# Three 256-column matmuls per step for the feature-major products, and gate products issued one column group early

## The chip, the cores and the metric

The kernel runs on one NeuronCore of a Trainium2 chip. The metric is the time of one execution on the device in microseconds (us); several executions give a median. Engines as the profile names them: PE is TensorE's matmul, PEld its weight load, DVE is VectorE, ACT is ScalarE, POOL is GpSimd, SP is SyncE (here it issues the DMAs of the weights). PSUM is the memory that matmuls write to, SBUF the one that all engines work in.

## The reference

One layer of a decoder trunk with four parallel branches, 256 positions (S), 2048 features (D), float32, and a final norm:

```python
h = rmsnorm(x, norm_g)
proj = jnp.einsum('bsd,df->bsf', h, w_in)            # 2048 x 18432
ya = stick_breaking_attention(a_q, a_k, a_v) * silu(a_g)
yb = conformer_conv(b_a, b_b, ...) * silu(b_g)
yc = spatial_gating(gelu(c_u), gelu(c_v), ...) * silu(c_g)
yd = dilated_mixture(d_q, d_k, d_v) * silu(d_g)
yproj = jnp.einsum('bsnc,ncd->bsnd', stack(ya, yb, yc, yd), w_branch)
gates = sigmoid(jnp.einsum('bsd,df->bsf', h, w_gate) + b_gate)
x = x + jnp.einsum('bsd,de->bse', sum(gates * yproj), w_out)
return rmsnorm(x, final_g)
```

The input projection has 14 column groups, named a_q, a_k and so on; each branch is 1024 wide. The gate has a 2048-column group for each branch.

## The kernel before

**Precision.** Large products run on numbers split in two: `hi` is the value rounded to the matmul's format (a ScalarE copy, L130), `lo` the rest (a VectorE subtraction, L131). A product is `hi*hi + lo*hi + hi*lo`, three terms added up in PSUM. Activations are split once (`xhl` holds h with its 256 hi columns beside its 256 lo columns; `y` likewise for a branch), weights as they arrive.

**Weights.** `weight_plan` lists 258 tiles of 128 x 2048 in the order of use. `next_weights` loads the next one (SP queue, three landing buffers) and splits it in two halves into five `hi` and five `lo` buffers, with a priority 300 instructions ahead of its place. A half is freed by the last matmul that reads it.

**Two kinds of product.** *Feature-major* (`unit_t`, `mm_t`): weights are the stationary operand, h the moving one, and the result has features on partitions. For each of 16 steps k, L245 multiplies the hi weights with all 512 columns of `xhl` (hi and lo of h), and L248 the lo weights with its 256 hi columns. A tile `ps` takes two such products in a 512-column half each; `evac` (L264) adds the two 256-column parts of each half, by a ScalarE copy (L266) and a VectorE addition (L267). 120 weight tiles go this way. *Token-major* (`mm_n`, L286 to L288): h or y is stationary, 512 weight columns move, and positions are on partitions. This is used for the value groups (`proj_n`), the gates (`psg`), the branch products (`psy`) and the output.

**Stages.** In order: d_v (`proj_v`, on x not yet normalized, with `make_h` producing h between its two column halves c=0 and c=1); b_a and b_b with the convolution, whose taps VectorE works off in the background; the dilated attention; then `gate_proj("d")`, b_g, `gate_proj("b")`, a_v and the stick-breaking attention, `gate_proj("a")`, c_v, c_u and c_g, `gate_proj("c")`, the output product and the final norm. `gate_proj` has four column groups c of 512; for each it makes the gate product (a bias matmul L369, then 96 matmuls), its sigmoid (L375), the branch product (48 matmuls), and multiplies and adds into `merged` (L382 to L385).

**Work put off.** `later(n, fn)` runs `fn` at the n-th next `tick()`; small steps of attention heads, and `sink` (transposes of a finished column group of `merged` into the operands `mh`, `ml` of the output product, L637), are emitted in the middle of later products in this way. `flush()` emits all that is pending at once.

**Order and buffers.** Python emits instructions in program order; a planner then orders each engine's instructions by priority and a simulated time, and gives tiles their buffers. A tile is freed when all that read or write it are done, and an engine takes its instructions in the planned order. PSUM has room for eight 512-column tiles: `ps_mm` two buffers of two (all large products), `ps_2` one buffer of two (`psy`, the norm's `pp`, attention's `po` and `cc`), `ps_s` two of one.

`make_h` (L213) uses `ps_2`: L225 and L226 sum the squares, L181 to L190 make `rstd`, sixteen L230 scale x, `split` makes `xhl`, L234 turns `rstd` into a column and L235 copies it out of `pp`.

Of the kernel before, what the change touches and what calls it, by code (L numbers as in the profile page):

```python
# [30 lines left out]
           c_u=7168, c_v=8192, c_g=9216, d_q=10240, d_k=13312, d_v=16384, d_g=17408)  # L31
BRANCH = dict(a=0, b=1, c=2, d=3)


def weight_plan():

    plan = []

    def t(name, i):
        plan.append(("in", OFF[name] // P + i))  # L40

    def n(name):
        for c in range(2):
            for q in range(4):
                plan.append(("inN", OFF[name] // 512 + c, q))

    def gate(b):
        for c in range(4):
            for q in range(4):
                plan.append(("gateN", BRANCH[b] * 4 + c, q))  # L50
            for q in range(2):
                plan.append(("brN", BRANCH[b], c, q))

    n("d_v")
    for i in range(8):
        t("b_a", i)
        t("b_b", i)
    for h in range(0, NH, 2):
        t("d_g", h)
        t("d_g", h + 1)  # L60
        for hh in (h, h + 1):
            for g in range(3):
                t("d_q", 8 * g + hh)
                t("d_k", 8 * g + hh)
    gate("d")
    for i in range(8):
        t("b_g", i)
    gate("b")
    n("a_v")
    for h in range(0, NH, 2):  # L70
        t("a_g", h)
        t("a_g", h + 1)
        for hh in (h, h + 1):
            t("a_q", hh)
            t("a_k", hh)
    gate("a")
    n("c_v")
    for i in range(8):
        t("c_u", i)
        t("c_g", i)  # L80
    gate("c")
    for c in range(4):
        for q in range(4):
            plan.append(("out", c, q))
    return plan
# [9 lines left out]
def hybrid_block(ctx: ExitStack, tc, w, x, xT, vec, bg, cst, dmask, sgu_wT, sgu_lg, sgu_lb, sgu_b, final_g, out):  # L95
# [11 lines left out]
    sc_p = ctx.enter_context(tc.tile_pool(name="sc", bufs=3))  # L107
    sm_p = ctx.enter_context(tc.tile_pool(name="sm", bufs=4))
    gt_p = ctx.enter_context(tc.tile_pool(name="gt", bufs=2))
    ps_mm = ctx.enter_context(tc.tile_pool(name="psm", bufs=2, space=bass.MemoryType.PSUM))  # L110
    ps_2 = ctx.enter_context(tc.tile_pool(name="ps2", bufs=1, space=bass.MemoryType.PSUM))
    ps_s = ctx.enter_context(tc.tile_pool(name="pss", bufs=2, space=bass.MemoryType.PSUM))

# [19 lines left out]
    def next_weights(expect, his=None, los=None):  # L133

        st = load_weights(expect)
        res = []
        for c in range(2):
            hi = his[c] if his else sp_p.tile([P, 1024], F32R, tag="hi", name="hi")[:]
            lo = los[c] if los else sp_p.tile([P, 1024], F32R, tag="lo", name="lo")[:]
            with tc.high_priority(SPLIT_AHEAD):  # L140
                split(hi, lo, st[:, c * 1024:(c + 1) * 1024])
            res.append((hi, lo))
        return res
# [3 lines left out]
    def later(n, fn):  # L147

        pending.append([n, fn])
# [11 lines left out]
    def flush():  # L161
        while pending:
            tick()
# [71 lines left out]
        V.tensor_copy(rstd_n[:], psn[:, 0:2])  # L235


    def mm_t(ps, j, weights, rhs, nk):

        for k in range(nk):  # L240
            hi, lo = weights[k // 8]
            o = (k % 8) * P

            def full(start, stop):
                T.matmul(ps[:, j, :], hi[:, o:o + P], rhs[:, k, :], start=start, stop=stop)  # L245

            def half():
                T.matmul(ps[:, j, 0:S], lo[:, o:o + P], rhs[:, k, 0:S], start=False, stop=False)  # L248

            if k < nk - 1:  # L250
                full(k == 0, False)
                half()
            else:
                half()
                full(False, True)

    def unit_t(e0, e1):
        ps = ps_mm.tile([P, 2, 512], F32, tag="mm", name="ps")
        mm_t(ps, 0, next_weights(e0), xhl, KD)
        mm_t(ps, 1, next_weights(e1), xhl, KD)  # L260
        tick()
        return ps

    def evac(ps, dst):  # L264
        bt = ev_p.tile([P, 2, S], F32, tag="bt", name="bt")
        A.activation(bt[:], ps[:, :, S:2 * S], AF.Copy)  # L266
        V.tensor_add(dst, ps[:, :, 0:S], bt[:])  # L267

    def ft(name, i):
        return ("in", OFF[name] // P + i)  # L270

    def proj_t(e0, e1):
        ps = unit_t(e0, e1)
        dst = qk_p.tile([P, 2, S], F32, tag="qk", name="dst")
        evac(ps, dst[:])
        return dst

    def mm_n(ps, weights, k0, lh, first, last, tbs=(0, 1)):
# [36 lines left out]
        return res  # L315

    def proj_n(name, c, step=None, first=False):
        ps = ps_mm.tile([P, 2, 512], F32, tag="mm", name="psn")
        for q in range(4):
            e = ("inN", OFF[name] // 512 + c, q)  # L320
            wts = first_weights(q, e) if first and c == 0 else next_weights(e)
            mm_n(ps, wts, 4 * q, xu_lh if first else x_lh, q == 0, q == 3)
            if q % 2:
                tick()
            if step is not None:
                step()
        if first and c == 0:
            make_h()
        return ps
# [25 lines left out]
        A.activation(bgr[:], b[:], AF.Copy)  # L355
        V.tensor_sub(bgr[32:64, :], b[32:64, :], bgr[32:64, :].bitcast(F32))

    def gate_proj(b, y, first=False, sink=None, step=None):

        bi = BRANCH[b]  # L360

        def y_lh(k, part, tb):
            return y[:, k, part * S + tb * P:part * S + (tb + 1) * P]

        for c in range(4):
            g = bi * 4 + c
            ps = ps_mm.tile([P, 2, 512], F32, tag="mm", name="psg")
            for tb in range(2):
                T.matmul(ps[:, tb, :], sel[:, g:g + 1].to_broadcast([P, P]), bgr[:], start=True, stop=False)  # L369
            for q in range(4):  # L370
                mm_n(ps, next_weights(("gateN", g, q)), 4 * q, x_lh, False, q == 3)
                if q % 2:
                    tick()
            gt = gt_p.tile([P, 2, 512], F32, tag="gt", name="gt")
            A.activation(gt[:], ps[:], AF.Sigmoid)  # L375
            psy = ps_2.tile([P, 2, 512], F32, tag="a2", name="psy")
            for q in range(2):
                mm_n(psy, next_weights(("brN", bi, c, q)), 4 * q, y_lh, q == 0, q == 1)
            tick()
            m = merged[:, :, c * 512:(c + 1) * 512]  # L380
            if first:
                V.tensor_mul(m, psy[:], gt[:])  # L382
            else:
                V.tensor_mul(gt[:], psy[:], gt[:])
                V.tensor_add(m, m, gt[:])  # L385
            if sink is not None:
                later(1, lambda c=c: sink(c))
            if step is not None:
                step()


    vd = proj_v("d_v", first=True)
# [80 lines left out]
            later(1, lambda g=g, qk=qk, qs=qs: scores(g, qk, qs))  # L473

    for h0 in range(0, NH, 2):
        sg = proj_t(ft("d_g", h0), ft("d_g", h0 + 1))
        A.activation(sg[:], sg[:], AF.Silu)
        conv(9)
        d_head(h0, sg)
        d_head(h0 + 1, sg)  # L480
# [24 lines left out]
                         scale=vec_sb[:, V_LG + i:V_LG + i + 1])  # L505

    conv_norm()
    flush()
    gate_bias()
    merged = big.tile([P, 2, D], F32, tag="m16", name="merged")  # L510
    gate_proj("d", yd, first=True)
# [2 lines left out]

    yb = new_y()
    for i in range(0, 8, 2):
        bg = proj_t(ft("b_g", i), ft("b_g", i + 1))
        A.activation(bg[:], bg[:], AF.Silu)
        V.tensor_mul(bg[:], bg[:], cv[:, i:i + 2, :])
        put_y(yb, i, 2, bg[:])  # L520

    flush()
    gate_proj("b", yb)


# [4 lines left out]
    ya = new_y()  # L530

    def a_pair(h0):
        sg = proj_t(ft("a_g", h0), ft("a_g", h0 + 1))
        A.activation(sg[:], sg[:], AF.Silu)
        zm = sc_p.tile([P, 2, 384], F32, tag="e1", bufs=1, name="zm")
        sph = sc_p.tile([P, 2, 384], F32R, tag="e3", bufs=1, name="sph")
        spl = sc_p.tile([P, 2, 384], F32R, tag="e4", bufs=1, name="spl")
# [41 lines left out]
    for h0 in range(0, NH, 2):  # L579
        a_pair(h0)  # L580

    flush()
    gate_proj("a", ya)


# [37 lines left out]
        put_y(yc, i, 1, ug[:, 0:1, :])  # L623

    for i in range(8):
        ug = proj_t(ft("c_u", i), ft("c_g", i))
        A.activation(ug[:, 0, :], ug[:, 0, :], AF.Gelu_apprx_tanh)
        A.activation(ug[:, 1, :], ug[:, 1, :], AF.Silu)
        later(2, lambda i=i, ug=ug: c_mix(i, ug))

    flush()


    mh = [t8_p.tile([P, KB, S], F32R, tag="t8", name=f"mh{i}") for i in range(2)]
    ml = [t8_p.tile([P, KB, S], F32R, tag="t8", name=f"ml{i}") for i in range(2)]

    def sink(c):  # L637
        pt = ps_mm.tile([P, 4, S], F32, tag="mm", name="pt")
        for f in range(4):
            for tb in range(2):  # L640
                o = c * 512 + f * P
                T.transpose(pt[:, f, tb * P:(tb + 1) * P], merged[:, tb, o:o + P], ident)
        ks = slice(4 * (c % 2), 4 * (c % 2) + 4)
        A.activation(mh[c // 2][:, ks, :], pt[:], AF.Copy)
        V.tensor_sub(ml[c // 2][:, ks, :], pt[:], mh[c // 2][:, ks, :].bitcast(F32))

    gate_proj("c", yc, sink=sink)
    flush()


    fg = y_p.tile([P, D], F32, tag="y", name="fg")
# [33 lines left out]
            (nc.scalar if c % 2 else nc.sync).dma_start(out[tb * P:(tb + 1) * P, cs], r[:, tb, cs])  # L685

    for c in range(3):
        ps = ps_mm.tile([P, 2, 512], F32, tag="mm", name="pso")
        for q in range(4):
            mm_n(ps, next_weights(("out", c, q)), 4 * q, m_lh, q == 0, q == 3)  # L690
        for tb in range(2):
            finish(c, ps, tb)
# [2 lines left out]
        wts.append(next_weights(("out", 3, q), his=[wh[:, q, 0, :], wh[:, q, 1, :]],  # L695
                                los=[sp_p.tile([P, 1024], F32R, tag="hi", name="wl")[:] for _ in range(2)] if q < 2 else None))
    for tb in range(2):
        ps = ps_mm.tile([P, 2, 512], F32, tag="mm", name="pso")
        for q in range(4):
            mm_n(ps, wts[q], 4 * q, m_lh, q == 0, q == 3, tbs=(tb,))  # L700
        finish(3, ps, tb)
        store(tb)
# [62 lines left out]
```

## Time and profile before

| | |
|---|---|
| median of 3 executions | 1505.41 us (1504.37 to 1506.78) |
| profiled execution | 1508.27 us, its span 1506.6 us |
| TensorE clock granted, mean | 0.994 |
| DMA | 280.47 MB, mean 186 GB/s |
| matmuls | 7484 |

The profile is of one execution and its times are in us from the start of the span. The first part gives each engine's busy time. "Idle before" is the time an engine stood still ahead of an instruction, with what ended it behind an arrow. Matmuls are pipelined: an entry's duration runs on while the next is already streaming, so the distance from start to start is what a matmul costs.

### The profile page before, as it was taken

The page shows a single profiled execution, that of the slowest core. Times are in us where ns is not written, and L with a number is a line of the kernel's source. Part 1 is how long each engine was busy: PE and PEld are TensorE (multiplying, and loading weights), DVE is VectorE, ACT ScalarE, POOL GpSimd, SP SyncE. Part 2 cuts the span into 40 slices and gives each one's busy share as a digit, 9 for nine tenths or more (in the row PEclk, how much of TensorE's full clock was granted, in tenths as well). Part 3 has the DMA queues.
Part 4 walks back from the last instruction along what each step waited for, and adds up shares of the span by engine and source line. Part 5 has one row for each costly group of instructions (what it writes and reads, how often), then busy time and mean ns, then how long its engine had stood idle before and what let it go on. Part 6 is the DMA issues. An engine that isn't in the chain of part 4 may idle for free.

```text
span 1506.6 us, 18648 instructions
## 1 busy us (share of the span) xinstructions
PE 1479.1 (98%) x7484; PEld 1255.4 (83%) x7484; DVE 944.4 (63%) x1249; ACT 760.2 (50%) x860; POOL 10.2 (1%) x22
## 2 busy tenths in 40 slices
PE   7999999999999999999999999999999999999997
PEld 5888888888888788888888888887888888888786
DVE  8899999866566754555545455554545666555454
ACT  7644445564454644454444466654444667444352
POOL 0000000000000000000000000000000000000000
PEclk9999999999999999999999999999999999999999
DMA  8555554445444555555555545444555555555562
GB/s 302 211 195 184 180 187 177 169 166 191 173 168 170 201 203 186 192 195 189 186 186 195 194 168 172 168 177 154 196 195 195 181 183 198 200 190 177 192 217 84
DMA packets 41318, 280.47 MB, mean 186 GB/s; under 512 B 4784, under 2 KB 4784, under 8 KB 8592
## 3 DMA queue, kind: packets, MB, share of 16 engines
q1 hardware_dynamic: 38880, 272.00, 50.5%
q0 software_dynamic: 1632, 6.24, 1.3%
q8 instruction: 58, 0.95, 0.3%
q10 hardware_dynamic: 720, 1.06, 0.2%
q14 instruction: 28, 0.23, 0.0%
HBM read 277.18 MB, written 2.10 MB: 185 GB/s over the span
## 4 chain that ended last, share of the span: by engine, by line
PE 97%; ACT 1%; DVE 1%; DMA 1%; issue 0%; DVEq 0%; ACTq 0%
PE ps L245 30%; PE ps L248 15%; PE psg L286 8%; PE psg L288 8%; PE psg L287 8%; PE psy L286 4%; PE psy L288 4%; PE psy L287 4%; PE psn L287 3%; PE psn L288 3%; PE psn L286 3%; PE pso L286 2%; PE pso L287 2%; PE pso L288 2%; DMA xt<-in_xT_dram 0%; PE psg L369 0%
## 5 line engine op out<-in xcount | busy, mean ns | idle before, releaser
L131 DVE TENSOR_TENSOR lo<-st,hi 128x1024 fp32r<-128x1024 f32 (+1 forms) x506 | 616.0, 1219 | 460.7 <-ACT hi L130 459.2
L130 ACT ACTIVATE hi<-st 128x1024 fp32r<-128x1024 f32 (+1 forms) x506 | 533.4, 1056 | 671.7 <-PE ps L245 262.3
L245 PE MATMUL ps<-xhl,hi 128*128 128x512 f32 x1920 | 675.5, 398 | 0.0
L248 PE MATMUL ps<-xhl,lo 128*128 128x256 f32 x1920 | 519.5, 281 | 0.0
L245 PEld LDWEIGHTS ps<-xhl,hi 128*128 128x128 f32 x1920 | 355.2, 188 | 74.6
L248 PEld LDWEIGHTS ps<-xhl,lo 128*128 128x128 f32 x1920 | 362.3, 189 | 9.6
L286 PE MATMUL psg<-hi,xhl 128*128 128x512 f32 x512 | 201.0, 393 | 1.1 <-ACT hi L130 1.1
L288 PE MATMUL psg<-hi,xhl 128*128 128x512 f32 x512 | 200.3, 391 | 0.0
L287 PE MATMUL psg<-lo,xhl 128*128 128x512 f32 x512 | 200.2, 391 | 0.0
L286 PEld LDWEIGHTS psg<-hi,xhl 128*128 128x128 f32 x512 | 96.4, 188 | 21.6 <-ACT hi L130 1.7
L288 PEld LDWEIGHTS psg<-hi,xhl 128*128 128x128 f32 x512 | 96.6, 189 | 20.2
L287 PEld LDWEIGHTS psg<-lo,xhl 128*128 128x128 f32 x512 | 96.6, 189 | 20.0
L412 DVE SCALAR_TENSOR_TENSOR cv<-glu,vec_sb,cv 128x255 f32<-128x255 f32 (+26 forms) x240 | 100.8, 463 | 0.2
L286 PE MATMUL psy<-hi,y 128*128 128x512 f32 x256 | 99.6, 389 | 0.0
L287 PE MATMUL psy<-lo,y 128*128 128x512 f32 x256 | 99.6, 389 | 0.0
L288 PE MATMUL psy<-hi,y 128*128 128x512 f32 x256 | 99.6, 389 | 0.0
L288 PEld LDWEIGHTS psy<-hi,y 128*128 128x128 f32 x256 | 48.1, 188 | 10.0
L287 PEld LDWEIGHTS psy<-lo,y 128*128 128x128 f32 x256 | 48.1, 188 | 10.0
L286 PEld LDWEIGHTS psy<-hi,y 128*128 128x128 f32 x256 | 48.1, 188 | 9.9
L286 PE MATMUL psn<-hi,xhl 128*128 128x512 f32 x128 | 49.8, 389 | 0.0
L287 PE MATMUL psn<-lo,xhl 128*128 128x512 f32 x128 | 49.8, 389 | 0.0
L288 PE MATMUL psn<-hi,xhl 128*128 128x512 f32 x128 | 49.8, 389 | 0.0
(207 smaller groups left out, 1105.2 us busy)
## 6 DMA issues: line engine op xcount, KB each, us to landing
st<-in_w_dram SPq DMA_DIRECT2D x254, 1024.0 KB, 4.8
xr<-in_x_dram POOLq DMA_DIRECT2D x8, 256.0 KB, 3.9
xt<-in_xT_dram SPq DMA_DIRECT2D x3, 512.0 KB, 8.7
st<-in_w_dram SPq DMA_DIRECT2D x4, 256.0 KB, 5.3
st<-in_w_dram SPq DMA_DIRECT2D x2, 512.0 KB, 7.4
fg<-in_final_g_dram POOLq DMA_DIRECT2D x1, 1024.0 KB, 6.8
out_dram<-r SPq DMA_DIRECT2D x4, 256.0 KB, 3.2
out_dram<-r ACTq DMA_DIRECT2D x4, 256.0 KB, 3.5
```

The lines of the kernel that those rows point to most:

```text
L130: A.activation(hi, src, AF.Copy)
L131: V.tensor_sub(lo, src, hi.bitcast(F32))
L245: T.matmul(ps[:, j, :], hi[:, o:o + P], rhs[:, k, :], start=start, stop=stop)
L248: T.matmul(ps[:, j, 0:S], lo[:, o:o + P], rhs[:, k, 0:S], start=False, stop=False)
L286: T.matmul(ps[:, tb, :], lh(k0 + kk, 0, tb), hi[:, o:o + 512], start=st, stop=False)
L287: T.matmul(ps[:, tb, :], lh(k0 + kk, 0, tb), lo[:, o:o + 512], start=False, stop=False)
L288: T.matmul(ps[:, tb, :], lh(k0 + kk, 1, tb), hi[:, o:o + 512], start=False, stop=sp)
L412: V.scalar_tensor_tensor(dst, src, wc, dst, op0=ALU.mult, op1=ALU.add)
```

## The change

- **Feature-major products.** Each step k is now three 256-column matmuls (hi weights with h's hi columns, hi weights with its lo columns, lo weights with its hi columns) that all add into the same 256 columns. Both products of a unit stand in one tile of 2 x 256 columns, from a new pool `ps_t` with two buffers. The sum is complete in PSUM, so one ScalarE pass evacuates it, with SiLU or GELU where one is wanted.
- **PSUM.** `ps_mm` goes from two buffers to one. Large token-major products alternate between `ps_mm` and `ps_2`: the second column half of `proj_n`, all `psy`, and every other output product take `ps_2`.
- **Gates.** `gate_proj` goes through `GATE_ORDER`: gate products g run one column group ahead of branch products y, and `sink` s stands at places of its own; the weight plan follows that order. The `flush()` calls around the gates are gone.
- **Transposes.** `sink` works in two parts of four transposes with tiles from `ps_t`; the one for the last column group is called in the first output product, ahead of its last quarter.

```diff
+GATE_ORDER = [(e[0], int(e[1])) for e in "g0 g1 y0 g2 s0 y1 g3 s1 y2 y3 s2".split()]
...
-    ps_mm = ctx.enter_context(tc.tile_pool(name="psm", bufs=2, space=bass.MemoryType.PSUM))
+    ps_t = ctx.enter_context(tc.tile_pool(name="pst", bufs=2, space=bass.MemoryType.PSUM))
+    ps_mm = ctx.enter_context(tc.tile_pool(name="psm", bufs=1, space=bass.MemoryType.PSUM))
...
+    def mm_t(ps, weights, rhs):
+
+        for k in range(KD):
             hi, lo = weights[k // 8]
             o = (k % 8) * P
...
+            T.matmul(ps, hi[:, o:o + P], rhs[:, k, 0:S], start=k == 0, stop=False)
+            T.matmul(ps, hi[:, o:o + P], rhs[:, k, S:2 * S], start=False, stop=False)
+            T.matmul(ps, lo[:, o:o + P], rhs[:, k, 0:S], start=False, stop=k == KD - 1)

     def unit_t(e0, e1):
-        ps = ps_mm.tile([P, 2, 512], F32, tag="mm", name="ps")
-        mm_t(ps, 0, next_weights(e0), xhl, KD)
-        mm_t(ps, 1, next_weights(e1), xhl, KD)
+        ps = ps_t.tile([P, 2, S], F32, tag="t", name="ps")
+        mm_t(ps[:, 0, :], next_weights(e0), xhl)
+        mm_t(ps[:, 1, :], next_weights(e1), xhl)
...
-    def proj_t(e0, e1):
+    def proj_t(e0, e1, funcs=(AF.Copy,)):
+
         ps = unit_t(e0, e1)
         dst = qk_p.tile([P, 2, S], F32, tag="qk", name="dst")
-        evac(ps, dst[:])
+        if len(funcs) == 1:
+            A.activation(dst[:], ps[:], funcs[0])
+        else:
+            for j in range(2):
+                A.activation(dst[:, j, :], ps[:, j, :], funcs[j])
...
     def proj_n(name, c, step=None, first=False):
-        ps = ps_mm.tile([P, 2, 512], F32, tag="mm", name="psn")
+        ps = (ps_2.tile([P, 2, 512], F32, tag="a2", name="psn") if c else
+              ps_mm.tile([P, 2, 512], F32, tag="mm", name="psn"))
...
+        def gate(c):
             g = bi * 4 + c
             ps = ps_mm.tile([P, 2, 512], F32, tag="mm", name="psg")
...
+            gts[c] = gt_p.tile([P, 2, 512], F32, tag="gt", name="gt")
+            A.activation(gts[c][:], ps[:], AF.Sigmoid)
+
+        def branch(c):
             psy = ps_2.tile([P, 2, 512], F32, tag="a2", name="psy")
...
+        for s, c in GATE_ORDER:
+            if s != "s":
+                (gate if s == "g" else branch)(c)
+            elif sink is not None:
+                sink(c)
...
     def sink(c):
-        pt = ps_mm.tile([P, 4, S], F32, tag="mm", name="pt")
...
+        for f0 in (0, 2):
+            pt = ps_t.tile([P, 2, S], F32, tag="t", name="pt")
...
     for c in range(3):
-        ps = ps_mm.tile([P, 2, 512], F32, tag="mm", name="pso")
+        ps = (ps_2 if c % 2 else ps_mm).tile([P, 2, 512], F32, tag="a2" if c % 2 else "mm", name="pso")
         for q in range(4):
+            if c == 0 and q == 3:
+                sink(3)
             mm_n(ps, next_weights(("out", c, q)), 4 * q, m_lh, q == 0, q == 3)
```

More of the change, by code (lines that the diff above doesn't have):

```diff
@@ L47, in gate @@
     def gate(b):
[L48 to L52, printed above, removed]
+        for s, c in GATE_ORDER:
+            if s == "g":
+                for q in range(4):
+                    plan.append(("gateN", BRANCH[b] * 4 + c, q))
+            elif s == "y":
+                for q in range(2):
+                    plan.append(("brN", BRANCH[b], c, q))
     n("d_v")
@@ L235, in make_h @@
         V.tensor_copy(rstd_n[:], psn[:, 0:2])
-    def mm_t(ps, j, weights, rhs, nk):
-        for k in range(nk):
+    def mm_t(ps, weights, rhs):
+        for k in range(KD):
             hi, lo = weights[k // 8]
             o = (k % 8) * P
[L244 to L255, printed above, removed]
+            T.matmul(ps, hi[:, o:o + P], rhs[:, k, 0:S], start=k == 0, stop=False)
+            T.matmul(ps, hi[:, o:o + P], rhs[:, k, S:2 * S], start=False, stop=False)
+            T.matmul(ps, lo[:, o:o + P], rhs[:, k, 0:S], start=False, stop=k == KD - 1)
     def unit_t(e0, e1):
-        ps = ps_mm.tile([P, 2, 512], F32, tag="mm", name="ps")
-        mm_t(ps, 0, next_weights(e0), xhl, KD)
-        mm_t(ps, 1, next_weights(e1), xhl, KD)
+        ps = ps_t.tile([P, 2, S], F32, tag="t", name="ps")
+        mm_t(ps[:, 0, :], next_weights(e0), xhl)
+        mm_t(ps[:, 1, :], next_weights(e1), xhl)
         tick()
         return ps
[L264 to L267, printed above, removed]
     def ft(name, i):
         return ("in", OFF[name] // P + i)
-    def proj_t(e0, e1):
+    def proj_t(e0, e1, funcs=(AF.Copy,)):
         ps = unit_t(e0, e1)
         dst = qk_p.tile([P, 2, S], F32, tag="qk", name="dst")
-        evac(ps, dst[:])
+        if len(funcs) == 1:
[3 more added lines that the diff above has]
+                A.activation(dst[:, j, :], ps[:, j, :], funcs[j])
         return dst
@@ L356, in gate_bias, with gate_proj @@
         V.tensor_sub(bgr[32:64, :], b[32:64, :], bgr[32:64, :].bitcast(F32))
-    def gate_proj(b, y, first=False, sink=None, step=None):
+    def gate_proj(b, y, first=False, sink=None):
         bi = BRANCH[b]
@@ L363, in y_lh @@
             return y[:, k, part * S + tb * P:part * S + (tb + 1) * P]
-        for c in range(4):
+        gts = {}
+        def gate(c):
             g = bi * 4 + c
@@ L373, in gate_proj @@
                     tick()
-            gt = gt_p.tile([P, 2, 512], F32, tag="gt", name="gt")
-            A.activation(gt[:], ps[:], AF.Sigmoid)
+            gts[c] = gt_p.tile([P, 2, 512], F32, tag="gt", name="gt")
+            A.activation(gts[c][:], ps[:], AF.Sigmoid)
+        def branch(c):
             psy = ps_2.tile([P, 2, 512], F32, tag="a2", name="psy")
@@ L379, in gate_proj @@
             tick()
-            m = merged[:, :, c * 512:(c + 1) * 512]
+            m, gt = merged[:, :, c * 512:(c + 1) * 512], gts.pop(c)
             if first:
@@ L385, in gate_proj @@
                 V.tensor_add(m, m, gt[:])
[L386 to L389, printed above, removed]
+        for s, c in GATE_ORDER:
+            if s != "s":
+                (gate if s == "g" else branch)(c)
+            elif sink is not None:
+                sink(c)
     vd = proj_v("d_v", first=True)
@@ L475, in hybrid_block @@
     for h0 in range(0, NH, 2):
-        sg = proj_t(ft("d_g", h0), ft("d_g", h0 + 1))
-        A.activation(sg[:], sg[:], AF.Silu)
+        sg = proj_t(ft("d_g", h0), ft("d_g", h0 + 1), (AF.Silu,))
         conv(9)
@@ L507, in hybrid_block @@
     conv_norm()
-    flush()
     gate_bias()
@@ L516, in hybrid_block @@
     for i in range(0, 8, 2):
-        bg = proj_t(ft("b_g", i), ft("b_g", i + 1))
-        A.activation(bg[:], bg[:], AF.Silu)
+        bg = proj_t(ft("b_g", i), ft("b_g", i + 1), (AF.Silu,))
         V.tensor_mul(bg[:], bg[:], cv[:, i:i + 2, :])
         put_y(yb, i, 2, bg[:])
-    flush()
     gate_proj("b", yb)
@@ L532, in a_pair @@
     def a_pair(h0):
-        sg = proj_t(ft("a_g", h0), ft("a_g", h0 + 1))
-        A.activation(sg[:], sg[:], AF.Silu)
+        sg = proj_t(ft("a_g", h0), ft("a_g", h0 + 1), (AF.Silu,))
         zm = sc_p.tile([P, 2, 384], F32, tag="e1", bufs=1, name="zm")
@@ L580, in hybrid_block @@
         a_pair(h0)
-    flush()
     gate_proj("a", ya)
@@ L625, in hybrid_block @@
     for i in range(8):
-        ug = proj_t(ft("c_u", i), ft("c_g", i))
-        A.activation(ug[:, 0, :], ug[:, 0, :], AF.Gelu_apprx_tanh)
-        A.activation(ug[:, 1, :], ug[:, 1, :], AF.Silu)
+        ug = proj_t(ft("c_u", i), ft("c_g", i), (AF.Gelu_apprx_tanh, AF.Silu))
         later(2, lambda i=i, ug=ug: c_mix(i, ug))
-    flush()
     mh = [t8_p.tile([P, KB, S], F32R, tag="t8", name=f"mh{i}") for i in range(2)]
@@ L637, in sink @@
     def sink(c):
-        pt = ps_mm.tile([P, 4, S], F32, tag="mm", name="pt")
[L639 to L645, printed above, removed]
+        for f0 in (0, 2):
+            pt = ps_t.tile([P, 2, S], F32, tag="t", name="pt")
+            for f in range(2):
+                for tb in range(2):
+                    o = c * 512 + (f0 + f) * P
+                    T.transpose(pt[:, f, tb * P:(tb + 1) * P], merged[:, tb, o:o + P], ident)
+            ks = slice(4 * (c % 2) + f0, 4 * (c % 2) + f0 + 2)
+            A.activation(mh[c // 2][:, ks, :], pt[:], AF.Copy)
+            V.tensor_sub(ml[c // 2][:, ks, :], pt[:], mh[c // 2][:, ks, :].bitcast(F32))
     gate_proj("c", yc, sink=sink)
-    flush()
     fg = y_p.tile([P, D], F32, tag="y", name="fg")
@@ L697, in hybrid_block @@
     for tb in range(2):
-        ps = ps_mm.tile([P, 2, 512], F32, tag="mm", name="pso")
+        ps = (ps_mm if tb else ps_2).tile([P, 2, 512], F32, tag="mm" if tb else "a2", name="pso")
         for q in range(4):
```

## The prediction

> **What bounds the kernel now.** I read the page from its first part to its chain, then the waits of TensorE, then the stretches of pure product work, then the timeline wherever TensorE stood still.
>
> ```profile
> span 1506.6 us, 18648 instructions
> PE 1479.1 (98%) x7484; PEld 1255.4 (83%) x7484; DVE 944.4 (63%) x1249; ACT 760.2 (50%) x860; POOL 10.2 (1%) x22
> PE 97%; ACT 1%; DVE 1%; DMA 1%; issue 0%; DVEq 0%; ACTq 0%
> L245 PE MATMUL ps<-xhl,hi 128*128 128x512 f32 x1920 | 675.5, 398 | 0.0
> L248 PE MATMUL ps<-xhl,lo 128*128 128x256 f32 x1920 | 519.5, 281 | 0.0
> ```
>
> TensorE is busy for 1479.1 of 1506.6 us and the chain that ends last is 97% TensorE. VectorE and ScalarE have 37% and 50% of the span to spare, so work taken from them is worth nothing unless TensorE waits for it. Two things can move the time: how long TensorE takes per product, and new or removed waits of TensorE. The idle column of L245 and L248 is 0.0: the feature-major products run without a gap.
>
> **Part A: three 256-column matmuls for one of 512 and one of 256.** There are 1920 steps k (120 weight tiles of 16). The columns stay the same (768), the matmuls go from two to three per step, each with its own weight load. What counts is the time from one matmul's start to the next, not the 398 and 281 ns, which overlap.
>
> ```profile
> 63.00:176.00 113.00, 113.00 (x641) 98.03 (x640) 104.45 (x184) 52.94 (x61) 0.00 (x0) 1.00 0.54 193
> 668.00:801.00 133.00, 133.00 (x588) 109.98 (x586) 68.03 (x58) 57.88 (x57) 0.00 (x0) 1.00 0.53 190
> ```
>
> These are two rows of the windows (stretch, length, TensorE busy with its count, weight loads, VectorE, ScalarE, GpSimd, clock). The first holds feature-major products alone: 113.00 us / 641 x 2 = 352.6 ns per step. The second holds token-major products alone: 133.00 / 588 = 226.2 ns for 512 columns. The next rows are the starts of weight tiles, 16 steps apart, and a place where 256-column matmuls follow one another:
>
> ```profile
> 68.41 0.63 PE L245 MATMUL ps<-xhl,hi 128*128 128x512 f32 x2
> 68.88 0.28 PE L248 MATMUL ps<-xhl,lo 128*128 128x256 f32 x1
> 68.99 0.40 PE L245 MATMUL ps<-xhl,hi 128*128 128x512 f32 x1
> 74.06 0.63 PE L245 MATMUL ps<-xhl,hi 128*128 128x512 f32 x2
> 187.84 0.28 PE L430 MATMUL s<-e,e 128*128 128x256 f32 x1
> 187.96 0.28 PE L431 MATMUL s<-e,e 128*128 128x256 f32 x1
> 188.08 0.28 PE L248 MATMUL ps<-xhl,lo 128*128 128x256 f32 x1
> 188.20 0.39 PE L245 MATMUL ps<-xhl,hi 128*128 128x512 f32 x1
> 240.57 0.64 PE L245 MATMUL ps<-xhl,hi 128*128 128x512 f32 x2
> 246.13 0.63 PE L245 MATMUL ps<-xhl,hi 128*128 128x512 f32 x2
> ```
>
> 74.06 - 68.41 = 5.65 us, or 353 ns per step; 246.13 - 240.57 = 5.56, or 347.5, which some tiles of the d, a and c branches reach. I take 352 for the mean. Three 256-column matmuls in a row take 188.20 - 187.84 = 0.36 us: 120 ns each. So a step becomes 3 x 120 = 360 ns, 8 ns more: **1920 x 8 = +15.4 us**. Bounds: a single one between two of 512 is followed after 0.11 (68.88 to 68.99) or 0.12; at 0.116, 3 x 116 = 348 gives -7.7 us; on the other side, if a step's two matmuls are 226.2 for the long one and the rest, 126.4, for the short one, three short ones take 379 ns, +52 us. I stay with the 0.36, the only row with three in succession.
>
> The Trainium skill (TensorE: Matmul & The Clock Gate, Back-to-back issue gap) puts a warm matmul at N/2.4 + 2.5 ns. By that estimate a step goes from 325 to 328 ns, +5 us; the 352.6 ns above disagree with it already.
>
> The evacuation loses 60 VectorE additions and several ScalarE passes. Both engines have the slack named above, and L245 never waits, so I cost it at 0; its cover is the 11 us that the next pair of tiles takes.
>
> **Part B: the second half of the d_v product moves into the buffer of the norm.** `proj_n` puts c=1 into `ps_2`, which has one buffer. In the first use `make_h` runs between c=0 and c=1 and holds that buffer (`pp`) until L235 has copied its last columns. Until then c=1 cannot begin; before, it had a buffer of its own. TensorE's order and VectorE's there:
>
> ```profile
> 34.60 0.39 PE L287 MATMUL psn<-lo,xuh 128*128 128x512 f32 x1
> 46.26 0.60 PE L234 MATMUL pp<-cst_sb,rstd 1*128 1x1 f32 x4
> 40.99 0.43 DVE L190 TENSOR_TENSOR rstd<-rstd,rs 128x256 f32<-128x256 f32 x1
> 42.76 6.42 DVE L230 SCALAR_TENSOR_TENSOR xt<-xt,vec_sb,rstd 128x256 f32<-128x256 f32 x16
> 50.23 1.22 DVE L131 TENSOR_TENSOR xhl<-xt,xhl 128x1024 fp32r<-128x1024 f32 x1
> 51.37 0.15 DVE L235 COPY rstd_n<-pp 128x2 f32<-128x2 f32 x1
> ```
>
> By count the 96 matmuls of c=0 end at the first row and c=1 starts near 35.0. With the release at 51.52, TensorE would stand for 16.5 us; if L234 and L235 came right behind L190 (41.42 + 0.60 + 0.15 = 42.2), for 7.2. In program order L235 stands behind the sixteen L230 and the splits of xhl, so it comes late; but VectorE is spared some 2.3 us of weight splits ahead of L190, since the split buffers are full while TensorE stands. 39.1 + 6.42 + 1.22 + 0.15 is 47: 12 us. All weight work queues behind it; nothing else for TensorE is ready, since the next products need xhl and weights that come later in the ring. Add the slow clock (part C), 1.6: **+13.5 us**, bounds +7 and +18.
>
> **Part C: one buffer where gate products had two.** `psg` now has one buffer and `psy` still one, and the order is g0 g1 y0 g2 s0 y1 g3 s1 y2 y3 s2. Most neighbours alternate, and a product of 11 to 22 us covers the eviction. Two don't: g1 waits for the sigmoid of g0, y3 for the multiplication of y2. Before, in the d branch, TensorE happened to meet the first wait:
>
> ```profile
> 505.94 0.39 PE L288 MATMUL psg<-hi,xhl 128*128 128x512 f32 x1
> 507.53 0.50 PE L286 MATMUL psg<-hi,xhl 128*128 128x512 f32 x1 [0.41 <-ACT hi L130]
> 506.41 1.06 ACT L130 ACTIVATE hi<-st 128x1024 fp32r<-128x1024 f32 x1 [0.48 <-ACT hi L130]
> 507.49 1.28 ACT L375 ACT_TABLE_LOAD   x1
> 508.79 1.02 ACT L375 ACTIVATE gt<-psg 128x1024 f32<-128x1024 f32 x1
> 509.86 0.73 PE L369 MATMUL psg<-bgr,sel 128*128 128x512 f32 x2 [1.83 <-ACT gt L375]
> 509.90:514.20 4.30, 4.30 (x12) 3.39 (x13) 2.79 (x3) 0.59 (x2) 0.00 (x0) 0.60 0.49 206
> L375 ACT ACT_TABLE_LOAD  x6: 1283/1283/1283, 507.5 to 1291.1; - x6
> 22.76 0.50 PE L287 MATMUL psn<-lo,xuh 128*128 128x512 f32 x1 [1.64 <-DVE lo L131]
> 23.10 0.39 PE L288 MATMUL psn<-hi,xul 128*128 128x512 f32 x1
> ```
>
> The last gate matmul starts at 505.94; ScalarE then does a weight split, a table load and the sigmoid, in that order, and the next bias matmul starts at 509.86. Against the usual 0.23 that is 3.7 us. After it the granted clock is 0.60, and 12 matmuls take 4.30 us instead of 12 x 0.226 = 2.7: another 1.6. Six of the 16 sigmoids have a table load in front of them (the row with x6), and the first gate of a branch follows other functions, so I charge 5.3 four times: +21.2. Without the table load it is 2.4 each, without the split too 1.35. Queued behind the bias matmul are the rest of g1 and y0; the split ring behind them fills and stops, with three tiles landed.
>
> ```profile
> L384 DVE TENSOR_TENSOR gt<-psy,gt 128x1024 f32<-128x1024 f32 x12 | 14.7, 1224 | 4.8 <-PE psy L288 4.8
> 1402.60 0.39 PE L288 MATMUL psy<-hi,y 128*128 128x512 f32 x1
> 1403.02 1.23 DVE L384 TENSOR_TENSOR gt<-psy,gt 128x1024 f32<-128x1024 f32 x1 [0.40 <-PE psy L288]
> 1312.28 0.87 PE pt L642 x8
> 1408.25 0.78 PE L286 MATMUL pso<-hi,mh 128*128 128x512 f32 x1
> ```
>
> For y3: VectorE is free when `psy` ends (0.4 us idle before each of 12), so y3 may start at 1403.02 + 1.23 = 1404.25 in such a place, 1.65 us after the last start, 1.4 more than usual: four times, +5.7, with no slow clock, as the wait of 1.64 us at 22.76 left the matmuls behind it at full pace (23.10, 0.39 long). **Part C: +26.9 us**; bounds +11 (no split, no table load, no slow clock) and +33 (slow clock at y3 too).
>
> The Trainium skill (TensorE: Matmul & The Clock Gate, Part 1) lets the clock fall to half after an idle window of about 3.4 us. Here 1.83 us, with the 0.41 at 507.53 ahead, was enough; by the page's window the 1.6 would be doubtful at g1, and part C up to 6.4 less.
>
> **Part D: what goes.**
>
> ```profile
> PE pt L642 <- DVE merged L385: 3.7, 1, 3.7
> PE psg L369 <- ACT gt L375: 3.7, 2, 1.8
> ```
>
> The first wait is the end of the last gate stage: from 1402.60 to 1408.25 are 5.65 us, of which 0.23 and 0.87 (eight transposes, as at 1312.28) are work; 4.6 go, and with them a slow clock as in part C, which I put at 1.2. The last column group's transposes now come after three quarters of the first output product (16 us), which cover both VectorE steps; but the fourth quarter then waits for a copy and a subtraction of 512 columns, about 0.8. Net -5. The second row's two waits (d and a branch) go with their slow clock and some 0.4 beside each (507.53): -3.9 each. **Part D: -12.8 us**, bounds -9 and -15. The same 32 transposes, 258 weight tiles and bytes remain; the later a_v, c_v and output products alternate between the two buffers, each covered by 11 us or more.
>
> **Sum.** 15.4 + 13.5 + 26.9 - 12.8 = +43.0 us. The profiled execution took 1508.27 (span 1506.6 and 1.7 around it), giving 1551; it lies 2.9 above the median of 1505.41, so the forecast is **1548 us**.
>
> **Rivals.**
> 1. *Faster.* The planner already moves matmuls across waits (the scores at 187.84 stand inside another product). If it puts ready work before the bias of g1 and before y3, and lets L234 and L235 through early, B and C shrink to about 4; with A at -7.7 and D at -12.8 the sum is -16.5: 1489. It decides where B + C fall below D less A. Against it: in the b branch no head is pending at the gate, and the next weights cannot be split while the ring is full.
> 2. *The short matmuls cost nothing* (117 to 118 ns each): 1548 - 15 = 1533. For it: the single gaps of 0.11 to 0.12. The page's spacing formula would land near it, at 1537.
> 3. *The start is not held up*, because the copy at L235 is placed early and c=1 waits little: 1548 - 13.5 = 1535. Against it: the buffer is one, and L235 stands last in program order.
> 4. *Both 2 and 3*: 1520.
> 5. *A weight load cannot hide behind 256 columns*, 126 ns each: 1548 + 36 = 1584. For it: loads are busy 98 of 113 us already. Against: the three in 0.36.
> 6. *The change gives back what it costs*: 2 and 3 hold and half of C is covered: about 1506.
>
> **Chances.** Forecast 0.42 (1538 to 1562); rival 1 0.15; 2 0.14; 3 0.14; 4 0.07; 5 0.05; 6 0.03. The range 1515 to 1564 takes in the forecast, 2, 3 and 4: 0.77. Measurements here tell 0.2% (3 us) from no change: faster 0.15, same 0.03, slower 0.82.
>
> **What would show it.** A: pure feature-major stretches at 360 ns per step, three equal gaps of 0.12. B: a TensorE wait for L235 between psn c=0 and c=1 of 7 to 17 us. C: a wait of the bias matmul for the sigmoid in each of four branches, 1.8 us or more, followed by a low clock, and a wait of 1.3 us for VectorE at y3. D: no wait of 3.7 us ahead of the output product. It is wrong if the short matmuls run below 117 ns, or if the waits of B and C are absent.

## The result, and the profile after

The changed kernel takes 1546.92 us (median of 4, 1544.26 to 1547.76), beside 1505.45 for the kernel before (1504.37 to 1506.78): 1.0272 times as long, 95% interval 1.0254 to 1.0290, or +41.5 us.

From the page of the changed kernel, its first part and the three feature-major groups (busy and mean ns behind the bar, then TensorE's idle time ahead of the group):

```profile
span 1544.8 us, 22382 instructions
PE 1500.0 (97%) x9404; PEld 1361.0 (88%) x9404; DVE 911.7 (59%) x1193; ACT 753.6 (49%) x845; POOL 10.3 (1%) x22
L248 PE MATMUL ps<-xhl,hi 128*128 128x256 f32 x1920 | 544.6, 284 | 0.7 <-ACT hi L135 0.7
L250 PE MATMUL ps<-xhl,lo 128*128 128x256 f32 x1920 | 543.3, 283 | 0.0
L249 PE MATMUL ps<-xhl,hi 128*128 128x256 f32 x1920 | 543.2, 283 | 0.0
```

The loss is in two places: TensorE is busy 20.9 us longer (1500.0 against 1479.1), and idle 17.3 us longer (44.8 of the span against 27.5). VectorE's 33 us less are worth nothing here, as the feature-major products had not waited for it. Where the idle time is, the longest waits of TensorE in the changed kernel show (who waits, for whom, us in total, times, longest):

```profile
PE psg L367 <- ACT gt L373: 11.2, 4, 3.5
PE psn L281 <- ACT xuh L214: 6.0, 1, 6.0
PE psn L281 <- DVE rstd_n L240: 5.6, 1, 5.6
PE pp L239 <- DVE rstd L195: 5.5, 1, 5.5
PE psn L282 <- DVE lo L136: 2.3, 2, 1.6
PE psn L281 <- ACT hi L135: 2.3, 2, 1.1
PE pso L281 <- ACT hi L135: 1.1, 1, 1.1
PE ps L248 <- ACT hi L135: 0.7, 1, 0.7
```

The two waits for the norm (5.6 and 5.5) are new. Of a gate's bias matmul for a sigmoid there are four waits, 11.2 us in all, where the kernel before had two, 3.7 in all. The 3.7 us ahead of the last transposes are gone. Setting the starts of the stages on TensorE side by side gives the account (us, changed less before):

| stage | before | changed | difference |
|---|---|---|---|
| start to first feature-major product | 57.34 | 71.22 | +13.9 |
| convolution and dilated attention, 72 tiles | 425.02 | 434.74 | +9.7 |
| b_g, a and c feature-major stages, 48 tiles | 284.56 | 290.49 | +5.9 |
| all else: gates, a_v, c_v, output product and end | | | +8.7 |

The third row adds up three stages, and the last is what is left of the 38.2 us between the spans; the medians differ by 3 us more, about what single executions scatter.

**The start.** TensorE and VectorE in the changed kernel's timeline (start, length, instruction, idle time ahead in brackets):

```profile
34.58 0.39 PE L283 MATMUL psn<-hi,xul 128*128 128x512 f32 x1
39.95 0.43 DVE L195 TENSOR_TENSOR rstd<-rstd,rs 128x256 f32<-128x256 f32 x1
40.41 6.42 DVE L235 SCALAR_TENSOR_TENSOR xt<-xt,vec_sb,rstd 128x256 f32<-128x256 f32 x16
40.43 1.01 PE L239 MATMUL pp<-cst_sb,rstd 1*128 1x1 f32 x4 [5.46 <-DVE rstd L195]
46.75 0.15 DVE L240 COPY rstd_n<-pp 128x2 f32<-128x2 f32 x1
47.05 0.76 PE L281 MATMUL psn<-hi,xuh 128*128 128x512 f32 x1 [5.61 <-DVE rstd_n L240]
71.22 0.28 PE L248 MATMUL ps<-xhl,hi 128*128 128x256 f32 x1
```

The copy that frees `pp` has its input from 41.4 on, but waits behind sixteen scalings until 46.75. The c=1 product begins at 47.05, where the kernel before had it near 35.0, and the first feature-major product at 71.22.

**A gate, b branch.** ScalarE, TensorE and the window behind the wait (the last three figures of the window's row are the granted clock, DMA's share and its GB/s):

```profile
715.04 0.39 PE L283 MATMUL psg<-hi,xhl 128*128 128x512 f32 x1
715.47 1.06 ACT L135 ACTIVATE hi<-st 128x1024 fp32r<-128x1024 f32 x1 [1.66 <-PE psg L283]
716.54 1.28 ACT L373 ACT_TABLE_LOAD   x1
717.83 1.02 ACT L373 ACTIVATE gt<-psg 128x1024 f32<-128x1024 f32 x1
718.91 1.22 PE L367 MATMUL psg<-bgr,sel 128*128 128x512 f32 x2 [3.48 <-ACT gt L373]
718.90:724.40 5.50, 5.49 (x13) 4.33 (x14) 0.00 (x0) 0.00 (x0) 0.00 (x0) 0.51 0.06 27
```

Split, table load and sigmoid stand in a row, 3.48 us of idle time; then the granted clock is 0.51 for 5.5 us, in which 13 matmuls run that need 2.9 at full clock. DMA falls to 0.06: the whole weight ring stands still with TensorE.

### The profile page after: what moved, and what is told of

The parts are those of the page before. It is cut to its first block, busy times and chain, and to the rows that moved or that the text cites. A ratio compares the mean times of both kernels' runs of the same rounds, so it can differ in the third digit from the quotient of the medians.

```text
span 1544.8 us, 22382 instructions
## 1 busy us (share of the span) xinstructions
PE 1500.0 (97%) x9404; PEld 1361.0 (88%) x9404; DVE 911.7 (59%) x1193; ACT 753.6 (49%) x845; POOL 10.3 (1%) x22
## 4 chain that ended last, share of the span: by engine, by line
PE 95%; ACT 2%; DVE 2%; DMA 1%; issue 0%; DVEq 0%; ACTq 0%
PE ps L248 15%; PE ps L250 15%; PE ps L249 15%; PE psg L281 8%; PE psg L282 8%; PE psg L283 8%; PE psy L283 4%; PE psy L281 4%; PE psy L282 4%; PE psn L281 2%; PE psn L282 2%; PE psn L283 2%; PE pso L281 2%; PE pso L283 2%; PE pso L282 2%; ACT hi L135 1%
## 5 line engine op out<-in xcount | busy, mean ns | idle before, releaser
L248 PE MATMUL ps<-xhl,hi 128*128 128x256 f32 x1920 | 544.6, 284 | 0.7 <-ACT hi L135 0.7
L250 PE MATMUL ps<-xhl,lo 128*128 128x256 f32 x1920 | 543.3, 283 | 0.0
L249 PE MATMUL ps<-xhl,hi 128*128 128x256 f32 x1920 | 543.2, 283 | 0.0
L248 PEld LDWEIGHTS ps<-xhl,hi 128*128 128x128 f32 x1920 | 368.3, 192 | 1.3 <-ACT hi L135 1.1
L249 PEld LDWEIGHTS ps<-xhl,hi 128*128 128x128 f32 x1920 | 368.2, 192 | 0.1
L250 PEld LDWEIGHTS ps<-xhl,lo 128*128 128x128 f32 x1920 | 368.2, 192 | 0.0
L414 DVE SCALAR_TENSOR_TENSOR cv<-glu,vec_sb,cv 128x239 f32<-128x239 f32 (+25 forms) x240 | 99.7, 462 | 0.2
L281 PE MATMUL psn<-hi,xhl 128*128 128x512 f32 x128 | 50.0, 391 | 2.3 <-ACT hi L135 2.3
```

The lines of the kernel that those rows point to most:

```text
L248: T.matmul(ps, hi[:, o:o + P], rhs[:, k, 0:S], start=k == 0, stop=False)
L249: T.matmul(ps, hi[:, o:o + P], rhs[:, k, S:2 * S], start=False, stop=False)
L250: T.matmul(ps, lo[:, o:o + P], rhs[:, k, 0:S], start=False, stop=k == KD - 1)
L281: T.matmul(ps[:, tb, :], lh(k0 + kk, 0, tb), hi[:, o:o + 512], start=st, stop=False)
L414: V.scalar_tensor_tensor(dst, src, wc, dst, op0=ALU.mult, op1=ALU.add)
```

## The experiments

Each was run beside the kernel before on its chip, whose medians were 1505.56 (first four), 1506.67 (next four) and 1505.57 (last two). Differences from the changed kernel are taken to its 1546.92; between sets of runs the medians of the kernel before differ by up to 1.2 us.

**1. The norm's sums in a pool of their own.**

```diff
-        pp = ps_2.tile([P, 2, 512], F32, tag="a2", name="pp")
-        pst, psn = pp[:, 0, :], pp[:, 1, :]
+        pst = ps_s.tile([P, 512], F32, tag="s", name="pp")
+        psn = ps_s.tile([P, 512], F32, tag="s", name="pn")
```

> The changed kernel, with the norm's two small sums in the one-bank pool ps_s, so that c=1 of the d_v product no longer waits for them; all else as changed. Theory (part B is a loss that nothing gives back): the first feature-major product starts near 57.5 us again in place of 71.2, and the whole falls by 13.9 us, to about 1533. Rival (the later stages make up for a late start, since the weight loads run further ahead): the start moves up but the whole falls by less than 5 us, to 1542 or more.

Measured: 1532.17 us, 14.7 less than the changed kernel. TensorE's timeline at the first feature-major product:

```profile
57.16 0.39 PE L283 MATMUL psn<-hi,xul 128*128 128x512 f32 x1
57.39 0.28 PE L249 MATMUL ps<-xhl,hi 128*128 128x256 f32 x1
```

57.4 in place of 71.2. What was lost at the start is nowhere given back. Part B is shown: 14.7 us by the medians, 13.9 by the start of the first feature-major product.

**2. The three matmuls alone, on the kernel before.**

```diff
-                T.matmul(ps[:, j, :], hi[:, o:o + P], rhs[:, k, :], start=start, stop=stop)
...
-                T.matmul(ps[:, j, 0:S], lo[:, o:o + P], rhs[:, k, 0:S], start=False, stop=False)
...
+            T.matmul(ps[:, j, 0:S], hi[:, o:o + P], rhs[:, k, 0:S], start=k == 0, stop=False)
+            T.matmul(ps[:, j, 0:S], hi[:, o:o + P], rhs[:, k, S:2 * S], start=False, stop=False)
+            T.matmul(ps[:, j, 0:S], lo[:, o:o + P], rhs[:, k, 0:S], start=False, stop=k == nk - 1)
...
-        bt = ev_p.tile([P, 2, S], F32, tag="bt", name="bt")
-        A.activation(bt[:], ps[:, :, S:2 * S], AF.Copy)
-        V.tensor_add(dst, ps[:, :, 0:S], bt[:])
+        A.activation(dst, ps[:, :, 0:S], AF.Copy)
```

> The kernel before, with only the feature-major step made of three 256-column matmuls and one ScalarE evacuation; buffers, order and transposes as before. Theory (120 ns a matmul, 360 a step against about 352): 1920 x 8.3 = +16 us, to about 1521, with steps of 360 ns in pure stretches. Rival (the 41 us are mostly the third matmul and its weight load, and the waits only replace older waits): +30 us or more, 1535 or above. Second rival (a single matmul of 256 is 116.7): -4 us, about 1501.

Measured: 1520.51 us, +15.0 on before (ratio 1.0101, 1.0084 to 1.0118). A window of feature-major products alone:

```profile
80.00:180.00 100.00, 100.00 (x836) 100.00 (x835) 96.32 (x180) 46.83 (x54) 0.00 (x0) 1.00 0.51 183
```

100.00 / 836 x 3 = 359 ns a step (the count takes in three matmuls that began before the window; without them it is 360). The evacuation that lost its addition gained nothing visible. Both rivals fall.

**3. A short matmul in the middle of each step.**

```diff
-            T.matmul(ps, hi[:, o:o + P], rhs[:, k, S:2 * S], start=False, stop=False)
+            T.matmul(ps[:, 0:P], hi[:, o:o + P], rhs[:, k, S:S + P], start=False, stop=False)
```

> The changed kernel, in which the second matmul of each feature-major step streams only 128 of its 256 columns (it leaves out the low part of h for positions 128 to 255). It tells what sets the 120 ns. If it is the columns plus a fixed cost (256 columns 106.7 + 13.3): the short one takes 66.7 and a step 307 ns, 1920 x 53 = -102 us, about 1445. If it is the weight load that each matmul has to wait for: the step stays at 360 ns and the time at about 1547. In between, a load that takes a fixed time below 120 shows as that time in the gap behind the short matmul.

Measured, one execution: 1525.27 us, 21.7 below the changed kernel where -102 or 0 were the two ends. TensorE's starts in a pure stretch:

```profile
80.17 0.28 PE L248 MATMUL ps<-xhl,hi 128*128 128x256 f32 x1
80.29 0.22 PE L249 MATMUL ps<-xhl,hi 128*128 128x128 f32 x1
80.35 0.33 PE L250 MATMUL ps<-xhl,lo 128*128 128x256 f32 x1
80.52 0.28 PE L248 MATMUL ps<-xhl,hi 128*128 128x256 f32 x1
```

The gap behind the short one is 0.06, but the next is 0.17, so the recorded start of L250 seems to run ahead of its work. From 80 to 180 us a step takes 348.9 ns on average; less two of 120 the short matmul costs 109. Half the columns saved 11 ns; at the rate from 512 columns to 256 (226 to 120 ns) they would have saved 53. What holds the short matmul up looks like the weight load: from one load's start to the next are 120.5, 118.9 and, behind the short matmul, 109.4 ns on average in this stretch. (A load is recorded as 190 ns long, but loads overlap.) The Trainium skill (TensorE: Matmul & The Clock Gate, LDWEIGHTS) puts a weight load at its columns divided by 1.2, an estimate of 107 ns for 128 columns. The 109 ns agree with it. That the load and no other cost per matmul sets the 109 ns is argued: no run leaves the load out. Either way, splitting a step into still shorter matmuls, each with its own load, would gain next to nothing here.

**4. Gate and branch products in turn.**

```diff
-GATE_ORDER = [(e[0], int(e[1])) for e in "g0 g1 y0 g2 s0 y1 g3 s1 y2 y3 s2".split()]
+GATE_ORDER = [(e[0], int(e[1])) for e in "g0 y0 g1 y1 s0 g2 y2 s1 g3 y3 s2".split()]
...
+            if s == "y" and c == 0:
+                flush()
```

> The changed kernel with the gate and branch products in turn (g0 y0 g1 y1 s0 g2 y2 s1 g3 y3 s2), what is pending emitted before y0; buffers as changed. Theory (the waits come from two products in a row in one buffer): the four waits of the bias matmul for the sigmoid and the wait ahead of y3 go, in the b branch 7.4 us and in the c branch about as much, while in d and a the pending heads may wait again ahead of y0 as they did before; in all -8 to -16 us, 1531 to 1539. Rival (one buffer for the gate product is short in any order): the waits move to other neighbours and the time stays within 4 us of 1547.

Measured: 1533.85 us, -13.1. From the waits of this run, those at the gates:

```profile
PE psg L367 <- ACT gt L373: 4.6, 2, 3.2
PE psg L282 <- DVE lo L136: 0.8, 1, 0.8
PE psy L281 <- DVE dst L468: 0.6, 1, 0.6
```

From first gate product to the next stage the b branch falls from 139.99 to 132.55 us, which is what the kernel before had. The waits in d and a stay, as expected. So in the b branch the neighbours in one buffer made the loss, not the single buffer as such.

**5. The changed order on the buffers of before.** Two buffers in `ps_mm`, 512 and 256 columns a step; order, weight plan, late `sink(3)` and removed `flush()` calls as in the change, and:

```diff
-            psy = ps_2.tile([P, 2, 512], F32, tag="a2", name="psy")
+            psy = (ps_mm if c == 3 else ps_2).tile([P, 2, 512], F32, tag="mm" if c == 3 else "a2", name="psy")
```

> The kernel before (two buffers for large products, 512 and 256 columns a step) with the changed order of the gates, the late transposes of the last column group, no emission of all pending work ahead of a gate, and y3 in the pool of two buffers. Theory (the order is good, its single buffers were the loss): no wait of g1 for the sigmoid, none ahead of y3, and the old waits of part D gone: -10 to -14 us against before, 1491 to 1496. Rival (the order itself brings waits, since g1 stands before y0 whatever the buffers): within 4 us of before, or slower.

Measured: 1495.65 us, ratio 0.9931 (0.9917 to 0.9944), -11.0. All its waits on TensorE behind the first product:

```profile
PE pso L291 <- ACT mh L651: 1.2, 1, 1.2
PE pso L293 <- DVE ml L652: 0.7, 1, 0.7
PE pso L291 <- DVE gt L393: 0.5, 1, 0.5
```

No gate waits. The order, with the late transposes and without the `flush()` calls, is a gain where each product has a free buffer; what each of the three is worth, this run does not separate.

**6. The late transposes alone, on the kernel before.**

```diff
-            if sink is not None:
+            if sink is not None and c < 3:
                 later(1, lambda c=c: sink(c))
...
+            if c == 0 and q == 3:
+                sink(3)
```

> The kernel before, with only the transposes of the last column group moved into the first output product, ahead of its last quarter. Theory: the wait of 3.7 us and its slow clock go, some 0.8 us comes back at the last quarter: -4 to -6 us, about 1500.5. Rival (the copy and subtraction are waited for there as long as before): within 1.5 us of before.

Measured: 1503.91 us, ratio 0.9982 (0.9973 to 0.9991), -2.8: faster, but short of the -4 to -6. Its waits show why:

```profile
PE pso L286 <- ACT mh L644: 1.2, 1, 1.2
PE pso L288 <- DVE ml L645: 0.7, 1, 0.7
```

1.9 us come back ahead of the last quarter, not 0.8.

**7. The sigmoid ahead of the weight split, on the changed kernel.**

```diff
-            A.activation(gts[c][:], ps[:], AF.Sigmoid)
+            with tc.high_priority(2 * SPLIT_AHEAD):
+                A.activation(gts[c][:], ps[:], AF.Sigmoid)
```

> The changed kernel, with the sigmoid of a gate given a higher priority than the weight split that stands ahead of it on ScalarE. Theory (the wait of g1 is split 1.06, table load 1.28, sigmoid 1.02 in a row): the split leaves the row, each of the four waits falls by up to 1.06 us, the total of 11.2 to about 7.5, and the time by 3 to 5 us, to about 1543; if the clock no longer falls, by up to 5 more. Rival (the wait is the sigmoid's own latency): no change, 1547.

Measured: 1532.47 us, -14.5, where I had expected 3 to 5 and at most 10 if the clock no longer falls. Timeline and window of the b branch, and the wait in all four branches:

```profile
710.44 1.28 ACT L374 ACT_TABLE_LOAD   x1
711.66 0.39 PE L283 MATMUL psg<-hi,xhl 128*128 128x512 f32 x1
712.08 1.02 ACT L374 ACTIVATE gt<-psg 128x1024 f32<-128x1024 f32 x1 [0.36 <-PE psg L283]
713.16 0.73 PE L367 MATMUL psg<-bgr,sel 128*128 128x512 f32 x2 [1.11 <-ACT gt L374]
713.00:718.00 5.00, 4.84 (x21) 4.03 (x22) 1.47 (x2) 2.12 (x3) 0.00 (x0) 1.00 0.44 184
PE psg L367 <- ACT gt L374: 3.1, 4, 1.1
```

The table load needs no data of the gate. It had been late only because it stood behind the split, which waits for the gate's last matmul; moved with the sigmoid, it runs under the gate product. The wait falls from 3.48 to 1.11 us (11.2 to 3.1 in all four), and the clock stays at 1.00. The mechanism was right, the size was not: I had left the table load in the row. The sum fits: 8.1 us of waiting are gone, and by the clock records of the changed kernel's trace TensorE worked 12.0 us at half clock behind the gate waits, which cost 6.0 us and do not occur in this run.

**8. Long and short matmuls grouped, on the kernel before.** For each half of a weight tile the eight short matmuls in a row, then the long ones (the very first long one ahead, as it starts the sum).

```diff
-        for k in range(nk):
...
+        for c in range(nk // 8):
+            if c == 0:
+                full(0)
+            for k in range(8 * c, 8 * c + 8):
+                half(k)
+            for k in range(max(8 * c, 1), 8 * c + 8):
+                full(k)
```

> The kernel before, with the feature-major matmuls of a weight half grouped: the eight of 256 columns in a row and the eight of 512 in a row, in place of turns; the same matmuls in all. Theory (each matmul costs its columns and 13.3 ns, 226.7 and 120, and turns of long and short add some 6 ns to most steps): steps fall from 352 to 347 ns, -8 to -10 us, about 1496. Rival (a long feature-major matmul costs 235 in any order, as two long ones in a row take 0.47): 355 ns a step, +5 us, about 1511.

Measured: 1502.39 us, ratio 0.9974 (0.9963 to 0.9985), -4.3: between the two theories. The starts of its groups (the last row is cut off by the end of the window):

```profile
83.37 2.23 PE L242 MATMUL ps<-xhl,hi 128*128 128x512 f32 x9
85.44 1.12 PE L246 MATMUL ps<-xhl,lo 128*128 128x256 f32 x8
86.39 1.78 PE L242 MATMUL ps<-xhl,hi 128*128 128x512 f32 x7
88.01 1.11 PE L246 MATMUL ps<-xhl,lo 128*128 128x256 f32 x8
88.96 1.32 PE L242 MATMUL ps<-xhl,hi 128*128 128x512 f32 x5
```

88.96 - 83.37 = 5.59 us for 16 steps, 349 ns each: 119 for a short one (0.95 / 8) and 230 for a long one (2.07 / 9). So taking turns costs some 4 ns a step here by the starts, and 2.2 by the time (4.3 us over 1920 steps). Why a long one takes 230 and not the 226 of the token-major products stays open.

**9. Runs 5 and 8 together.**

> The kernel before with both gains found so far: the order, late transposes and y3 buffer of the run on the buffers of before (-11 us), and the matmuls of a weight half grouped by length (-4 us). Theory (they act in different stages and add up): 1506 - 15 = 1491, 0.990 of before. Rival (grouping holds the low halves of the weights longer and the new order needs them sooner): no better than 1495.

Measured: 1492.57 us, ratio 0.9908 (0.9894 to 0.9923): 13.0 us below the kernel before and 54 below the changed one, the fastest found. Of the fifteen hoped for, two are missing; run 9 beats run 5 by some 3.

**10. Runs 1 and 7 together, on the changed kernel.**

> The changed kernel with the norm's sums in their own pool and the sigmoid ahead of the weight split, both at once; the three 256-column matmuls stay. Theory (the parts add up): 1546.9 - 14.7 - 14.5 = 1517.7, which leaves +12 on the kernel before: the 15 of part A less what the new order and the late transposes save. Rival (the two waits share a cause, the late weight ring): 1523 or more.

Measured: 1518.07 us, where the sum of the parts gave 1517.7; +12.5 on before. The two losses are independent. What is left would be the 15.0 of the three matmuls less a small gain of order and late transposes, in which the waits that stay (3.1 us for the sigmoid, some 4 at y3) are already counted; no run separates these.

## Why the prediction was right

The forecast was 1548 us, the median 1546.92. That the sum fits within 1 us owes something to luck, as terms erred in opposite ways (C + D is what run 1 and run 2 leave of the whole):

| term | predicted | measured | by |
|---|---|---|---|
| A, three matmuls a step | +15.4 | +15.0 | run 2 |
| B, the start | +13.5 | +14.7 | run 1 |
| C + D, gates and output | +14.1 | +11.8 | 41.5 - 15.0 - 14.7 |

- **A** rested on one spot in the trace with three short matmuls in a row. It held everywhere: 302 gaps of each kind between 60 and 180 us in the changed kernel have a mean of 120.0 ns. The lower bound (116) was read from single gaps, and run 3 shows how far a recorded start can run ahead of the work; the upper (126.4) took a long matmul at 226.2, where run 8 shows 230. Rivals 2, 4 and 5 fall, and with 2 also 6.
- **B**: the release was put at 47, with `rstd` ready at 39.1. They were 46.9 and 40.4; VectorE did the sixteen scalings with no split of `xhl` between them, so the one error cancelled the other. The slow clock behind the long wait was there: from 47.05 to 51.91 it was 0.50, and 12 matmuls took 4.86 us where they need 2.7, a loss of some 2 us in place of 1.6. Rival 3 falls.
- **C**, first wait: right in its place and in its three pieces (split, table load, sigmoid). Its size is 3.1 to 3.5 us in d, b and c, and 1.4 in a, where the sums of the last heads stood in the gap, with no slow clock after it. In b the slow clock lasted 5.5 us, longer than the 4.30 it was priced on. The four were charged 21.2. Run 7 took 14.5 of it away and left four waits of at most 1.1 us, or 3.1 in all, which makes about 18.
- **C**, second wait: no matmul of y3 appears among the waits, and the step named it wrongly. The planner put a matmul of the next product ahead of y3, and that one waits for a weight split. In the changed kernel's timeline, d branch:

```profile
634.88 0.39 PE L283 MATMUL psy<-hi,y 128*128 128x512 f32 x1
635.31 1.23 DVE L382 TENSOR_TENSOR merged<-psy,gt 128x1024 f32<-128x1024 f32 x1 [0.40 <-PE psy L283]
636.42 0.39 PE L248 MATMUL ps<-xhl,hi 128*128 128x256 f32 x1 [0.69 <-ACT hi L135]
636.76 0.40 PE L281 MATMUL psy<-hi,y 128*128 128x512 f32 x1
```

  y3 starts 1.88 us after the last of y2, where 1.65 was charged, and four useful matmuls stand between. The multiplication ends at 636.54, so here the price is much the same with either waiter. The waits at these four places (0.7, two that make 2.3, and 1.1) add up to 4.1 us, where 5.7 was charged.
- **D**: the waits it named are gone and none is in their place in the output product of the changed kernel. Alone (run 6) the late transposes gave 2.8 where 5 was charged, as 1.9 us came back there. The whole of D, with the order, is seen in run 5: -11.0 against -12.8. If D is worth as much in the changed kernel, C alone is 11.8 + 11.0 = 22.8, where 26.9 was forecast: both were put too large, and the two errors in part made up for each other.

Rival 1, the faster one, asked for B + C to be covered by other work. The planner covered about 2 us, in the a branch.

## What to carry to other kernels

Before splitting a matmul, read the start-to-start distance of the shorter one where several follow each other, not its duration and not a single gap; in this stream half the columns saved only 11 of 120 ns. When a pool loses a buffer, go through every pair of neighbours in the order that shares it, the one-time ones at the start too, and price the whole eviction with what stands ahead of it on its engine; afterwards look for the piece that could have run earlier, such as the table load of run 7. An order and the buffers that it needs are judged together: the same order with its late transposes cost 12 us with one buffer and gained 11 with two.

## What the runs showed of the hardware

- A matmul of 128 columns with its own weight load took 109 ns in this stream (run 3), one of 256 columns 120 (run 2), one of 512 from 226 (token-major windows of the kernel before) to 230 (run 8): between 128 and 256 columns the price hardly falls.
- The granted clock fell to about half behind each wait of 3.1 to 3.5 us. Behind shorter ones it depended on the execution: behind 1.43 us in the a branch it did not fall in the changed kernel, but fell in run 1, and behind 1.83 in the d branch it fell in the kernel before, but not in run 2. A wait and the window behind it, first of run 1, then of run 2:

```profile
1039.87 0.74 PE L367 MATMUL psg<-bgr,sel 128*128 128x512 f32 x2 [1.43 <-ACT gt L373]
1040.90:1044.30 3.40, 3.40 (x10) 2.65 (x9) 0.00 (x0) 1.06 (x2) 0.00 (x0) 0.50 0.00 0
519.68 0.73 PE L357 MATMUL psg<-bgr,sel 128*128 128x512 f32 x2 [1.83 <-ACT gt L363]
519.60:524.00 4.40, 4.32 (x19) 3.58 (x20) 1.90 (x2) 4.37 (x9) 0.82 (x1) 1.00 0.85 303
```

  So the loss behind a short wait is no fixed price. By the clock records each low stretch behind a gate wait lasted 3.41 or 6.83 us. Where the clock falls, a wait is worth more than its own length: in run 7 the waits fell by 8.1 us and the time by 14.5.
